# Norm scales of the feed-forwards by two matrix products, copies and offsets of activation rows, and a last down unit by halves, in a two-layer decoder trunk

## Chip, cores and metric

The kernel runs on one core of one Trainium2 chip. The metric is the device time of one execution in microseconds; the median of three runs is quoted. The core's engines are called PE (TensorE), DVE (VectorE), ACT (ScalarE), POOL (GpSimd) and SP (SyncE, which issues nearly all transfers).

## The reference

All of it is float32, with 256 tokens and a width of 1024:

```python
def rms_norm(x, g):
    return x * rsqrt(mean(x * x, axis=-1) + 1e-6) * g

# layer 0
x = x + short_conv_mixer(rms_norm(x, a_norm), ...)      # width-3 causal convolution, gates
x = x + conv_glu_ffn(rms_norm(x, f_norm[0]), ...)       # 1024 -> 2 x 2816 -> 1024
k, v = (rms_norm(x, kv_norm) @ w for w in (w_k, w_v))
# layer 1
x = x + attention(rms_norm(x, b_norm) @ w_q, k, v, rel_bias) @ w_o   # 16 heads of 64, causal
x = x + conv_glu_ffn(rms_norm(x, f_norm[1]), ...)
return rms_norm(x, final_norm)

def conv_glu_ffn(h, w_up, conv_w, conv_b, w_down):
    u = causal_dwconv(h @ w_up, conv_w) + conv_b        # width 3
    g, v = split(u, 2)
    return (silu(g) * v) @ w_down
```

## The kernel before

**Layout and precision.** x is held transposed: 8 row tiles of 128 features by 256 tokens (`xT`). Every float32 matrix product is made of three products in the float32r format: a weight w is split into `hi` (a rounding copy by ACT, L92) and `lo` (the rest, by DVE, L98), an activation into `xh`, `xl` in the same way, and `mm3` (L166) issues wh·xh, wh·xl, wl·xh. Nearly all of PE's work are such products of a 128x128 weight tile with 256 columns. `psum` holds 4 banks `acc` for down projections, 3 banks `up`, and one `misc`.

**Weights** come in units: a big one (`B`, 1 MB) holds two times 8 tiles of an up, query/key or value projection, a small one (`S`, 0.5 MB) a row of a down or output projection. Three raw buffers and three split buffers ("slots") for each size rotate. `hi(tag)` and `lo(tag)` split the next unit in line, whole or by parts; when the last part of a `lo` is done, the load of the unit three further is issued on SP. `hi` is only issued where the slot's previous unit has been used. The order on every engine is the order in which the program is written.

**The norm's scale isn't applied to x.** The products run on x times the gain, and the rows' scale 1/rms is multiplied into the results as they leave PSUM. So PE can start on a new projection before the scale is known. `boundary` (L293) adds the last projection to x, splits x into `xh`, `xl`, squares it on ACT and adds the squares up on DVE to one 128x256 tile `sq[:, 2, :]`. `rstd_cols` (L323) sums that over the partitions with two one-column fp32 products (L327), so that the tokens lie on partitions, and takes the root in three Newton steps on 128x2 (L312 to L317). It makes diagonal matrices of it (L335), and `rstd_rows` (L338) turns those with one fp32 product with a matrix of ones (L341) into a row of 256 scales on every partition, which ACT copies to `rr`. An fp32 product is issued as two in the trace.

**Feed-forward** (`ffn`, L494): 22 units. Unit i multiplies x with its up tiles into a bank of `up` (48 products), `conv` (L498) takes the bank out times `rr` into `u` (DVE, L502), makes the convolution's first tap on ACT (L509) and the other two on DVE (L377), with weight splits between them, and `gate` (L517) makes silu (ACT), `hid` (DVE) and its parts `sh` (ACT) and `sl` (DVE). The `sl` of a unit is issued in the `conv` of the next one, behind its `u` (L504). The down products of unit i (24) stand three units later on PE (L553). Layer 0 has features on the partitions (`down_bank`), layer 1 tokens (`token_bank`: hh·hi, hh·lo, hl·hi). In unit 1 the products run over rows 1, 2, 3, then `rstd_cols`, then the rows 0 and 4 to 7, then `rstd_rows`. Row 0 is taken from a copy, `xh.again`, `xl.again` (`tile_0_again`, L266), that lies 128 bytes into its tile, while the rows themselves begin 192 bytes into a multiple of 512 (`Rows`, L252).

**Attention.** Units v0, v1, v2, q0 to q7, v3 in this order. A query/key unit has products with `xqh` and `xvh` in turn (`qk_step`, L600). Behind every second one a `group` of four heads follows with fp32 scores (L643), softmax, transposes of the group before and its fp32 products with v (L699). The heads' outputs lie in `oh` and `ol`, 8 rows one behind the other (`shifted`, L247). The output projection `wo` has 8 units of 24 products: rows 0 and 1, transposes of the last group, row 2, its products with v, rows 3 to 7.

**The end.** The last unit of layer 1 has its down weights split in `gate(last)`: `hi("S")`, silu, the first half of `lo`, `hid`, `sh`, the second half, `sl`. `token_last` runs the last three units' down products.

Of the kernel before, what the change touches and what calls it, by code (L numbers as in the profile page):

```python
# [17 lines left out]
S = 256  # L18
D = 1024
# [18 lines left out]
def f32(ap):  # L38
    return ap.bitcast(F32)
# [3 lines left out]
def yoco_kernel(ctx: ExitStack, tc: tile.TileContext, t: dict, out: bass.AP):  # L43
# [202 lines left out]

    def shifted(pool, name, tag, rows, **kw):  # L247

        t = pool.tile([128, rows * S + 64], F32R, name=name, tag=tag, **kw)
        return t[:, 48:48 + rows * S].rearrange("p (k s) -> p k s", s=S)  # L250

    class Rows:  # L252
# [7 lines left out]
        def __getitem__(self, i):  # L260
            return self.rows[i]

    def parts_tiles():
        return Rows("xh"), Rows("xl")

    def tile_0_again(xh, xl):  # L266
        A.activation(xh.again, f32(xh[:, 0, :]), AF.Copy)
        V.tensor_copy(xl.again, f32(xl[:, 0, :]))

    def scaled_hi(x, gain, ks, xh, order=same):  # L270
# [67 lines left out]
    def rstd_rows(dg, scales=(1.0,), orders=(same,)):  # L338
# [6 lines left out]
        return r  # L345


    ext_d = dram.tile([NH, 384], F32, name="ext_d")
# [15 lines left out]
    def bias_pair(j):  # L364
# [3 lines left out]
        return b  # L368

    def split_act(src, n, at=64):  # L370

        h, lw = (tmp.tile([128, 384 + 64], F32R, name="s" + x, tag="z" + x, bufs=4)[:, at // 4:at // 4 + n]
                 for x in "hl")
        return (h, lw), lambda: A.activation(h, src, AF.Copy), lambda: V.tensor_sub(lw, src, f32(h))  # L374

# [111 lines left out]
    xh, xl, sq = boundary(acc, xT, P_FN)  # L487
    tile_0_again(xh, xl)
    hi("S")

# [3 lines left out]
    def ffn(layer, xh, xl, sq, bank=down_bank, between=None):  # L494
# [3 lines left out]
        def conv(j, last=False):  # L498
# [6 lines left out]
            if not last:  # L505
                lo("B")
            o = tmp.tile([128, 2, S], F32, name="cv", bufs=2)
# [9 lines left out]
        def gate(j, o, last=False):  # L517
            sl = tmp.tile([128, S], F32, name="sl", tag="sc", bufs=4)
            hi("S")
            A.activation(sl, o[:, 0, :], AF.Silu)  # L520
            lo("S", 0, 1 + last)
            hid = tmp.tile([128, S], F32, name="hid", tag="pr", bufs=4)
            V.tensor_mul(hid, sl, o[:, 1, :])  # L523
            hd[j], zh, low[j] = split_act(hid, S, 64 if layer == 0 else 128)
            zh()
            if last:
                lo("S", 1, 2)
                low[j]()

        acc = None  # L530
        for i in range(FJ):
# [27 lines left out]
            if i == 0:  # L559
                hi("B")  # L560
        if bank is token_bank:
# [9 lines left out]

    xvh, xvl, sq = boundary(acc, xT, P_KVN, rev)
    xqh, xql = parts_tiles()
    vs = wpool.tile([128, 2, D], F32, name="vs", tag="hiB2")
    oh = None
    ol = shifted(act, "ol", "ol", KT, bufs=1)
    vb, qb, qs, sb, pr, pt, ps_, ob, bias = {}, {}, {}, {}, {}, {}, {}, {}, {}
# [21 lines left out]

    def qk_step(j, ks=range(KT)):  # L600
        u = WH["q", j]
        assert u.lo is not None
        wh, wl = u.v(u.hi, 2), u.v(u.lo, 2)
        for k in ks:
            mm3(qb[j][:, 0, :], wh[:, k, 0, :], wl[:, k, 0, :], xqh[:, k, :], xql[:, k, :],
                start=(k == 0), stop=(k == KT - 1))
            mm3(qb[j][:, 1, :], wh[:, k, 1, :], wl[:, k, 1, :], xvh[:, k, :], xvl[:, k, :],
                start=False, stop=(k == KT - 1))
        u.used = ks[-1] == KT - 1
# [128 lines left out]
    for kind, n in heads:  # L738
        if kind == "v":
            vb[n] = acc_bank() if n < 3 else up_bank()  # L740
            if n == 1:
                v_step(1, range(0, 4))
                ycol, dg = rstd_cols(sq)
                v_step(1, range(4, 8))
                oh = shifted(act, "oh", "oh", KT, bufs=1)
            elif n == 2:
# [26 lines left out]
        else:  # L773
            qb[n] = up_bank()
            qk_step(n)
            if n % 2:
# [4 lines left out]
            else:  # L781
                qk_out(n)
                if n:
                    fin[1]()
                hi("B")
                lo("B")
# [27 lines left out]
    xh, xl, sq = boundary(acc, xT, P_FN + KT)  # L814
    tile_0_again(xh, xl)
    hi("S")

# [115 lines left out]
```

## Time and profile before

| | |
|---|---|
| median of 3 runs | 573.8 us (573.79, 573.80, 574.29) |
| profiled execution, its own time | 574.54 us |
| its span, first to last instruction | 572.8 us |
| granted TensorE clock, mean over the span | 0.999 |
| PE, PE's weight loads, DVE, ACT, POOL busy | 98%, 97%, 81%, 58%, 2% of the span |
| products on PE | 4924 |
| read from HBM | 106.65 MB, 188 GB/s over the span |

The profile's instruction times are microseconds from the span's start. A busy share says how long an engine had an instruction in it; matmuls overlap, so PE's share says little of its speed, and the distance from one start to the next is the thing to look at. The chain that ended last is the list of what each step waited for, back from the end.

The span divides into the mixer (to 95.2 us), layer 0's feed-forward (to about 278), values, queries and keys and attention (to 358), the output projection (to 383.9), layer 1's feed-forward (to 566) and the final norm.

### The profile page before, as it was taken

Reading aid. Unit: us, or ns where it says so; the run is one execution under the profiler, and the core shown is the slowest. Engines: PE = TensorE matmul, PEld = TensorE weight load, DVE = VectorE, ACT = ScalarE, POOL = GpSimd, SP = SyncE. Lnnn points to the kernel's source line nnn. Section 1 sums busy time; section 2 is a strip of 40 time slices with the busy share of each in tenths; the row PEclk is TensorE's granted clock in tenths of the full one; section 3 lists DMA queues with packets and bytes.
Section 4 is the critical chain, followed back from the end, with each engine's and each line's share of the span. In section 5 each row is a group of like instructions: output and inputs, shape, how many; then the busy total and the mean of one; then the engine's idle time right before and its main releaser. Section 6 shows DMA issues by size and latency. Waiting matters only on the chain.

```text
span 572.8 us, 11802 instructions
## 1 busy us (share of the span) xinstructions
PE 563.2 (98%) x4924; PEld 557.8 (97%) x4924; DVE 464.8 (81%) x786; ACT 334.6 (58%) x502; POOL 12.2 (2%) x33
## 2 busy tenths in 40 slices
PE   8999999999999999999999999999999999999995
PEld 7999999999999999999999999999999999999994
DVE  5998869888877787777978888658999988888865
ACT  7765437566665566555765666456566556555443
POOL 0410000000000000000000000000000000000001
PEclk9999999999999999999999999999999999999999
DMA  8986583537445644564265655444656554563111
GB/s 286 398 290 218 181 298 112 185 133 264 179 168 215 221 170 168 215 221 156 103 220 196 221 195 189 138 170 148 221 184 221 221 195 162 196 221 129 57 38 73
DMA packets 24180, 108.47 MB, mean 189 GB/s; under 512 B 2736, under 2 KB 5440, under 8 KB 16192
## 3 DMA queue, kind: packets, MB, share of 16 engines
q1 hardware_dynamic: 23840, 107.43, 52.4%
q8 instruction: 38, 0.62, 0.4%
q10 hardware_dynamic: 288, 0.30, 0.2%
q14 instruction: 14, 0.11, 0.1%
HBM read 106.65 MB, written 1.07 MB: 188 GB/s over the span
## 4 chain that ended last, share of the span: by engine, by line
PE 95%; DVE 1%; ACT 1%; DMA 1%; SPq 0%; issue 0%; POOLq 0%; POOL 0%; ACTq 0%
PE up L167 19%; PE up L168 19%; PE up L169 19%; PE acc L167 7%; PE acc L168 7%; PE acc L169 7%; PE acc L198 3%; PE acc L196 3%; PE acc L197 3%; PE up L699 1%; PE acc L588 1%; DMA xres<-xT 1%; PE acc L590 1%; PE acc L591 1%; PE acc L643 1%; DVE loB L98 1%
## 5 line engine op out<-in xcount | busy, mean ns | idle before, releaser
L167 PE MATMUL up<-xh,hiB 128*128 128x256 f32 x944 | 262.2, 278 | 0.7 <-ACT hiB L92 0.6
L169 PE MATMUL up<-xh,loB 128*128 128x256 f32 x944 | 261.1, 277 | 0.5 <-DVE loB L98 0.5
L168 PE MATMUL up<-xl,hiB 128*128 128x256 f32 x944 | 260.9, 276 | 0.0
L167 PEld LDWEIGHTS up<-xh,hiB 128*128 128x128 f32 x944 | 177.2, 188 | 1.6 <-ACT hiB L92 1.1
L169 PEld LDWEIGHTS up<-xh,loB 128*128 128x128 f32 x944 | 177.4, 188 | 0.9 <-DVE loB L98 0.9
L168 PEld LDWEIGHTS up<-xl,hiB 128*128 128x128 f32 x944 | 177.2, 188 | 0.1
L98 DVE TENSOR_TENSOR loB<-rawB,hiB 128x2048 fp32r<-128x2048 f32 (+2 forms) x76 | 147.6, 1948 | 5.3 <-ACT hiB L92 5.0
L92 ACT ACTIVATE hiB<-rawB 128x2048 fp32r<-128x2048 f32 (+1 forms) x73 | 123.5, 1696 | 22.6 <-issue 10.1
L98 DVE TENSOR_TENSOR loS<-rawS,hiS 128x1024 fp32r<-128x1024 f32 (+2 forms) x73 | 83.6, 1146 | 11.5 <-ACT hiS L92 11.2
L509 ACT ACTIVATE cv<-u,pk 128x256 f32<-128x256 f32 x88 | 48.2, 595 | 71.2 <-DVE u L502 71.2
L377 DVE SCALAR_TENSOR_TENSOR cv<-u,pk,cv 128x255 f32<-128x255 f32 x192 | 81.3, 478 | 2.7 <-ACT cv L509 1.7
L92 ACT ACTIVATE hiS<-rawS 128x1024 fp32r<-128x1024 f32 (+1 forms) x71 | 71.6, 1010 | 10.2 <-PE acc L168 6.3
L502 DVE TENSOR_TENSOR u<-up,rr 128x512 f32<-128x512 f32 x44 | 30.3, 689 | 45.2 <-PE up L169 43.8
L169 PE MATMUL acc<-sh,loS 128*128 128x256 f32 x240 | 66.2, 276 | 0.0
L167 PE MATMUL acc<-sh,hiS 128*128 128x256 f32 x240 | 66.2, 276 | 0.0
L168 PE MATMUL acc<-sl,hiS 128*128 128x256 f32 x240 | 66.2, 276 | 0.0
L374 ACT ACTIVATE sh<-hid 128x256 fp32r<-128x256 f32 x52 | 21.7, 417 | 60.0 <-DVE hid L523 55.2
L198 PE MATMUL acc<-hiS,sl 128*128 128x256 f32 x176 | 48.7, 277 | 0.0
L196 PE MATMUL acc<-hiS,sh 128*128 128x256 f32 x176 | 48.7, 277 | 0.0
L197 PE MATMUL acc<-loS,sh 128*128 128x256 f32 x176 | 48.6, 276 | 0.0
L169 PEld LDWEIGHTS acc<-sh,loS 128*128 128x128 f32 x240 | 45.1, 188 | 0.0
L168 PEld LDWEIGHTS acc<-sl,hiS 128*128 128x128 f32 x240 | 45.0, 188 | 0.0
(151 smaller groups left out, 751.9 us busy)
## 6 DMA issues: line engine op xcount, KB each, us to landing
rawB<-w_up SPq DMA_DIRECT2D x44, 1024.0 KB, 4.8
rawS<-w_dn SPq DMA_DIRECT2D x44, 512.0 KB, 3.4
rawB<-w_qk SPq DMA_DIRECT2D x8, 1024.0 KB, 4.8
rawB<-w_mc SPq DMA_DIRECT2D x6, 1024.0 KB, 8.0
rawS<-w_mo SPq DMA_DIRECT2D x8, 512.0 KB, 4.5
rawB<-w_v SPq DMA_DIRECT2D x4, 1024.0 KB, 4.8
rawS<-w_o SPq DMA_DIRECT2D x8, 512.0 KB, 3.6
rawS<-w_mb SPq DMA_DIRECT2D x7, 512.0 KB, 5.3
```

The source lines that it names most:

```text
L92: A.activation(self.hi[:, c], self.raw[:, c], AF.Copy)
L98: V.tensor_sub(self.lo[:, c], self.raw[:, c], f32(self.hi[:, c]))
L167: PE.matmul(o, wh, xh, start=start, stop=False, skip_group_check=True)
L168: PE.matmul(o, wh, xl, start=False, stop=False, skip_group_check=True)
L169: PE.matmul(o, wl, xh, start=False, stop=stop, skip_group_check=True)
L196: PE.matmul(o, hh[:, tok], u.hi[:, f], start=(first and d.start == 0), stop=False, skip_group_check=True)
L197: PE.matmul(o, hh[:, tok], u.lo[:, f], start=False, stop=False, skip_group_check=True)
L198: PE.matmul(o, hl[:, tok], u.hi[:, f], start=False, stop=last, skip_group_check=True)
L374: return (h, lw), lambda: A.activation(h, src, AF.Copy), lambda: V.tensor_sub(lw, src, f32(h))
L377: V.scalar_tensor_tensor(o[:, back:], u[:, :S - back], w, o[:, back:], op0=OP.mult, op1=OP.add)
L502: V.tensor_mul(u, ub[j], rr[:, 0:1, :].to_broadcast([128, 2, S]))
L509: A.activation(o[:, half, :], u[:, half, :], AF.Identity, scale=cw[half][2], bias=par(P_FCB, c0 + half * FJ))
```

## The change

- **`each`**, a 128x128 float32r matrix of 1/1024, 192 bytes into a tile, is made at the start by ACT.
- **`boundary`** with `split` (both feed-forwards; not the keys and values) splits the sum of squares into `sh`, `sl` parts too, and splits the next big unit's `lo` half before, half behind the sums. `tile_0_again` stands in it now.
- **`rstd_direct`** replaces `rstd_cols` and `rstd_rows` in both feed-forwards. Two products with `each` as the stationary tile and the parts as moving ones give the mean of squares in a row on every partition, in `misc`; DVE adds epsilon and takes the root there, with two steps that have other constants: ten operations on 128x256. No ACT copy is left.
- **Unit 1** runs over rows 1 to 6, the norm's two products, the copy of row 0, and row 7.
- **The next big unit** is split by ACT in halves behind unit 0; DVE's first half of `lo` comes before the norm, the second in `conv(0)`.
- **`Heads`** replaces `shifted`: of the heads' output rows, row 3 lies 192 bytes and rows 4 to 7 lie 256 bytes further on.
- **Queries and keys:** behind unit 0's output, row 0 of both inputs is copied, and unit 2 takes row 0 from the copies.
- **The last unit** has ACT's `hi("S")` in two halves, one before and one behind silu.

```diff
+    each = const.tile([128, 192], F32R, name="each")[:, 48:176]
...
+    A.activation(each, ones, AF.Copy, scale=1.0 / D)
...
+    class Heads:
...
+        def __getitem__(self, i):
+            p, j, s = i
...
+            at = 48 + j * S + (48 if j == 3 else 64 if j > 3 else 0)
+            return self.t[p, at:at + S][:, s]
...
-    def boundary(acc, x, gain, order=same):
+    def boundary(acc, x, gain, order=same, split=True):
...
         sum_squares(sq, 0)
-        for part in range(2):
-            lo("B", part, 2)
-        sum_squares(sq, 1, order)
+        if split:
+            lo("B", 0, 2)
+            sum_squares(sq, 1, order)
+            sq, high, low = split_act(sq[:, 2, :], S)
+            high()
+            lo("B", 1, 2)
+            low()
+            tile_0_again(xh, xl)
...
+    def rstd_direct(parts):
+        ps = psum.tile([128, 512], F32, name="misc", bufs=1)
+        PE.matmul(ps[:, :S], each, parts[0], start=True, stop=False, skip_group_check=True)
+        PE.matmul(ps[:, :S], each, parts[1], start=False, stop=True, skip_group_check=True)
+        r = act.tile([128, 2, S], F32, name="rr", bufs=1)
+        w = tmp.tile([128, 2, S], F32, name="u", bufs=2)
+        ms, a, y = w[:, 0, :], w[:, 1, :], r[:, 0, :]
+        V.tensor_scalar(ms, ps[:, :S], EPS, None, op0=OP.add)
+        V.tensor_scalar(y.bitcast(I32), ms.bitcast(I32), -0.5, float(0x5F1FFFF9), op0=OP.mult, op1=OP.add)
+        V.tensor_mul(a, y, y)
+        V.scalar_tensor_tensor(a, a, -0.703952253, ms, op0=OP.mult, op1=OP.mult)
+        V.scalar_tensor_tensor(y, a, 0.703952253 * 2.38924456, y, op0=OP.add, op1=OP.mult)
+        V.tensor_mul(a, y, y)
+        V.tensor_mul(a, a, ms)
+        V.tensor_scalar(ms, a, 0.375, -1.25, op0=OP.mult, op1=OP.add)
+        V.tensor_mul(a, ms, a)
+        V.scalar_tensor_tensor(y, a, 1.875, y, op0=OP.add, op1=OP.mult)
+        return r
...
             if not last:
-                lo("B")
+                lo("B", *((1, 2) if j == 0 else ()))
...
-            hi("S")
+            hi("S", 0, 1 + last)
             A.activation(sl, o[:, 0, :], AF.Silu)
             lo("S", 0, 1 + last)
+            if last:
+                hi("S", 1, 2)
...
-                up_step(up[1], ub[1], xh, xl, 2, range(1, 4), first=1)
-                _, dg = rstd_cols(sq)
+                up_step(up[1], ub[1], xh, xl, 2, range(1, 7), first=1)
+                rr = rstd_direct(sq)
                 lo("S")
                 A.activation(first, ones[:, 0:1], AF.Silu)
-                up_step(up[1], ub[1], xh, xl, 2, (0, 4, 5, 6, 7), first=1, again=True)
-                rr = rstd_rows(dg)
+                up_step(up[1], ub[1], xh, xl, 2, (0, 7), first=1, again=True)
...
             if i == 0:
-                hi("B")
+                for part in range(2):
+                    hi("B", part, 2)
+                hi("S")
+                lo("B", 0, 2)
...
+            for i, (h, lw) in enumerate(((xqh, xql), (xvh, xvl))):
+                h, lw = (h.again, lw.again) if again and k == 0 else (h[:, k, :], lw[:, k, :])
...
-            qk_step(n)
+            qk_step(n, again=n == 2)
...
+                else:
+                    tile_0_again(xqh, xql)
+                    tile_0_again(xvh, xvl)
```

The order of DVE from the sums of squares of layer 0's feed-forward on, before (`nw` holds the root's terms on 128x2, `sq` the squares; two more rounds like the last three rows follow):

```order
L98 TENSOR_TENSOR loB_1313<-rawB,hiB_1161 128x1024 x2
L285 TENSOR_TENSOR sq<-sq 128x512
L287 TENSOR_TENSOR sq<-sq 128x512
L288 TENSOR_TENSOR sq<-sq 128x256
L268 CAST xl<-xl 128x256
L331 TENSOR_SCALAR nw<-misc 128x2
L312 TENSOR_SCALAR nw<-nw 128x2
L314 TENSOR_TENSOR nw<-nw 128x2
L316 SCALAR_TENSOR_TENSOR nw<-nw 128x2
L317 SCALAR_TENSOR_TENSOR nw<-nw 128x2
```

and the same place now, as far as the norm's first operation (`sl<-sq,sh` is the low part of the sum of squares; line numbers are those of the changed kernel):

```order
L98 TENSOR_TENSOR loB_1315<-rawB,hiB_1163 128x1024
L303 TENSOR_TENSOR sq<-sq 128x512
L305 TENSOR_TENSOR sq<-sq 128x512
L306 TENSOR_TENSOR sq<-sq 128x256
L98 TENSOR_TENSOR loB_1315<-rawB,hiB_1163 128x1024
L286 TENSOR_TENSOR sl<-sq,sh 128x256
L280 CAST xl<-xl 128x256
L98 TENSOR_TENSOR loB_1384<-rawB,hiB_1379 128x1024
L384 TENSOR_SCALAR u<-misc 128x256
```

Half a weight split has moved behind the sums, and the low part and half of the next unit's split stand before the norm.

Further on in DVE's order, between the norm and `u` of unit 0, before:

```order
L335 TENSOR_SCALAR dg<-ident,nw 128x128 x2
L98 TENSOR_TENSOR loS_1414<-rawS,hiS_1323 128x1024
L502 TENSOR_TENSOR u<-up,rr 128x512
L98 TENSOR_TENSOR loB_1455<-rawB,hiB_1375 128x2048
L377 SCALAR_TENSOR_TENSOR cv<-u,pk,cv 128x255 x2
```

and now:

```order
L385 TENSOR_SCALAR rr<-u 128x256
L386 TENSOR_TENSOR u<-rr 128x256
L387 SCALAR_TENSOR_TENSOR u<-u 128x256
L388 SCALAR_TENSOR_TENSOR rr<-u,rr 128x256
L389 TENSOR_TENSOR u<-rr 128x256
L390 TENSOR_TENSOR u<-u 128x256
L391 TENSOR_SCALAR u<-u 128x256
L392 TENSOR_TENSOR u<-u 128x256
L393 SCALAR_TENSOR_TENSOR rr<-u,rr 128x256
L98 TENSOR_TENSOR loS_1438<-rawS,hiS_1382 128x1024
L543 TENSOR_TENSOR u<-up,rr 128x512
L98 TENSOR_TENSOR loB_1384<-rawB,hiB_1379 128x1024
```

The root's operations are 256 columns wide, the small unit's split still stands between them and `u`, and only half a big split is left behind `u`. Layer 1 has the same order.

## Rows read from the trace of the kernel before

**Rows 1.** The page, part 4: shares of the chain that ended last, by engine.

```profile
PE 95%; DVE 1%; ACT 1%; DMA 1%; SPq 0%; issue 0%; POOLq 0%; POOL 0%; ACTq 0%
```

**Rows 2.** Stretches: us, busy (instructions) of PE, PEld, DVE, ACT, POOL; PEclk, DMA, GB/s.

```profile
120.00:250.00 130.00, 130.00 (x1149) 130.00 (x1149) 102.66 (x152) 76.94 (x102) 0.00 (x0) 1.00 0.53 194
371.00:383.50 12.50, 12.50 (x108) 12.50 (x107) 6.42 (x10) 5.71 (x7) 0.00 (x0) 1.00 0.64 212
306.60:317.60 11.00, 11.00 (x96) 11.00 (x95) 10.08 (x26) 6.12 (x18) 0.00 (x0) 1.00 0.51 168
```

**Rows 3.** Chain that ended last, units 1 and 2 of layer 0: start, us, what.

```profile
102.85 0.34 PE misc L327 x4
103.19 0.23 PE up L167
...
104.00 0.12 PE up L167
...
104.35 0.11 PE up L167
...
106.73 0.43 PE misc L341 x2
```

**Rows 4.** Timeline of PE, layer 0: start, us, instruction; unit 1's start, first down product.

```profile
100.64 0.28 PE L167 MATMUL up<-xh,hiB 128*128 128x256 f32 x1
...
117.91 0.28 PE L167 MATMUL acc<-sh,hiS 128*128 128x256 f32 x1
```

**Rows 5.** Timeline of DVE, 102 to 115 us, from the norm to unit 0's `sl`.

```profile
103.22 0.16 DVE L331 TENSOR_SCALAR nw<-misc 128x2 f32<-128x2 f32 x1 [0.50 <-PE misc L327]
103.42 0.17 DVE L312 TENSOR_SCALAR nw<-nw 128x2 int32<-128x2 int32 x1
...
107.62 0.69 DVE L502 TENSOR_TENSOR u<-up,rr 128x512 f32<-128x512 f32 x1 [0.61 <-ACT rr L344]
...
110.42 1.66 DVE L377 SCALAR_TENSOR_TENSOR cv<-u,pk,cv 128x255 f32<-128x255 f32 x4
112.23 1.23 DVE L98 TENSOR_TENSOR loS<-rawS,hiS 128x1024 fp32r<-128x1024 f32 x1
...
114.31 0.41 DVE L374 TENSOR_TENSOR sl<-hid,sh 128x256 fp32r<-128x256 f32 x1
```

**Rows 6.** Timeline of ACT, 107 to 114 us, the splits behind the first tap.

```profile
109.34 1.90 ACT L92 ACTIVATE hiB<-rawB 128x2048 fp32r<-128x2048 f32 x1
111.15 1.05 ACT L92 ACTIVATE hiS<-rawS 128x1024 fp32r<-128x1024 f32 x1
```

**Rows 7.** Groups of DVE by shape: count, busy us, mean ns, idle before and releasers.

```profile
L377 DVE SCALAR_TENSOR_TENSOR cv<-u,pk,cv 128x255 f32<-128x255 f32 x96 | 42.8, 479 | 2.4 <-ACT cv L509 1.7 <-ACT cv L415 0.6
...
L523 DVE TENSOR_TENSOR hid<-sl,cv 128x256 f32<-128x256 f32 x44 | 18.5, 419 | 2.2 <-ACT sl L520 2.0
...
L671 DVE TENSOR_SCALAR pr<-pr,st 128x256 f32<-128x256 f32 x16 | 5.6, 351 | 0.3
...
L316 DVE SCALAR_TENSOR_TENSOR nw<-nw 128x2 f32<-128x2 f32 x12 | 1.9, 162 | 0.4
...
L598 DVE TENSOR_SCALAR vs<-acc,nw 128x256 f32<-128x256 f32 x3 | 1.3, 476 | 0.0
```

**Rows 8.** Timeline of PE, units 0 and 1 of layer 1.

```profile
383.85 0.28 PE L167 MATMUL up<-xh,hiB 128*128 128x256 f32 x1
...
391.51 0.28 PE L169 MATMUL up<-xh,loB 128*128 128x256 f32 x1
392.19 0.58 PE L327 MATMUL misc<-ones,sq 128*128 128x1 f32 x4 [0.40 <-DVE sq L288]
```

**Rows 9.** Timelines of ACT and PE at layer 1's last down unit.

```profile
557.31 1.06 ACT L92 ACTIVATE hiS<-rawS 128x1024 fp32r<-128x1024 f32 x1 [0.90 <-PE acc L198]
...
559.72 0.28 PE L198 MATMUL acc<-hiS,sl 128*128 128x256 f32 x1
...
560.42 0.38 PE L198 MATMUL acc<-hiS,sl 128*128 128x256 f32 x1
560.65 0.28 PE L196 MATMUL acc<-hiS,sh 128*128 128x256 f32 x1
```

More of the change, by code (lines that the diff above doesn't have):

```diff
@@ L245, in same @@
         return a
-    def shifted(pool, name, tag, rows, **kw):
-        t = pool.tile([128, rows * S + 64], F32R, name=name, tag=tag, **kw)
-        return t[:, 48:48 + rows * S].rearrange("p (k s) -> p k s", s=S)
     class Rows:
@@ L261, in __getitem__, with __init__ @@
             return self.rows[i]
+    class Heads:
+        def __init__(self, name):
+            self.t = act.tile([128, KT * S + 128], F32R, name=name, bufs=1)
+        def __getitem__(self, i):
+            p, j, s = i
+            if isinstance(j, slice):
+                at = 48 + j.start * S + (64 if j.start > 3 else 0)
+                n = S + 48 if j.start == 2 else S
+                return self.t[p, at:at + 2 * n].rearrange("p (a s) -> p a s", s=n)[:, :, 0:S][:, :, s]
+            at = 48 + j * S + (48 if j == 3 else 64 if j > 3 else 0)
+            return self.t[p, at:at + S][:, s]
     def parts_tiles():
@@ L268, in tile_0_again, with split_act @@
         V.tensor_copy(xl.again, f32(xl[:, 0, :]))
+    def split_act(src, n, at=64):
+        h, lw = (tmp.tile([128, 384 + 64], F32R, name="s" + x, tag="z" + x, bufs=4)[:, at // 4:at // 4 + n]
+                 for x in "hl")
+        return (h, lw), lambda: A.activation(h, src, AF.Copy), lambda: V.tensor_sub(lw, src, f32(h))
     def scaled_hi(x, gain, ks, xh, order=same):
@@ L304, in boundary @@
         sum_squares(sq, 0)
-        for part in range(2):
-            lo("B", part, 2)
-        sum_squares(sq, 1, order)
+        if split:
[8 more added lines that the diff above has]
+            for part in range(2):
+                lo("B", part, 2)
+            sum_squares(sq, 1, order)
         return xh, xl, sq
@@ L368, in bias_pair @@
         return b
[L370 to L374, printed above, removed]
     def tap(o, u, w, back):
@@ L487, in yoco_kernel @@
     xh, xl, sq = boundary(acc, xT, P_FN)
-    tile_0_again(xh, xl)
-    hi("S")
     LAG = 3
@@ L518, in gate @@
             sl = tmp.tile([128, S], F32, name="sl", tag="sc", bufs=4)
-            hi("S")
+            hi("S", 0, 1 + last)
             A.activation(sl, o[:, 0, :], AF.Silu)
             lo("S", 0, 1 + last)
+            if last:
+                hi("S", 1, 2)
             hid = tmp.tile([128, S], F32, name="hid", tag="pr", bufs=4)
@@ L559, in ffn @@
             if i == 0:
-                hi("B")
+                for part in range(2):
+                    hi("B", part, 2)
+                hi("S")
+                lo("B", 0, 2)
         if bank is token_bank:
@@ L569, in yoco_kernel @@
     acc = ffn(0, xh, xl, sq)
-    xvh, xvl, sq = boundary(acc, xT, P_KVN, rev)
+    xvh, xvl, sq = boundary(acc, xT, P_KVN, rev, split=False)
     xqh, xql = parts_tiles()
@@ L575, in yoco_kernel @@
     oh = None
-    ol = shifted(act, "ol", "ol", KT, bufs=1)
+    ol = Heads("ol")
     vb, qb, qs, sb, pr, pt, ps_, ob, bias = {}, {}, {}, {}, {}, {}, {}, {}, {}
@@ L598, in v_out, with qk_step @@
         V.tensor_scalar(vs[:, 1, cols], vb[n][:, 1, :], ycol[:, 1:2], None, op0=OP.mult)
-    def qk_step(j, ks=range(KT)):
+    def qk_step(j, ks=range(KT), again=False):
         u = WH["q", j]
@@ L604, in qk_step @@
         for k in ks:
[L605 to L608, printed above, removed]
+            for i, (h, lw) in enumerate(((xqh, xql), (xvh, xvl))):
+                h, lw = (h.again, lw.again) if again and k == 0 else (h[:, k, :], lw[:, k, :])
+                mm3(qb[j][:, i, :], wh[:, k, i, :], wl[:, k, i, :], h, lw,
+                    start=(k == 0 and i == 0), stop=(k == KT - 1))
         u.used = ks[-1] == KT - 1
@@ L744, in yoco_kernel @@
                 v_step(1, range(4, 8))
-                oh = shifted(act, "oh", "oh", KT, bufs=1)
+                oh = Heads("oh")
             elif n == 2:
@@ L784, in yoco_kernel @@
                     fin[1]()
+                else:
+                    tile_0_again(xqh, xql)
+                    tile_0_again(xvh, xvl)
                 hi("B")
@@ L814, in yoco_kernel @@
     xh, xl, sq = boundary(acc, xT, P_FN + KT)
-    tile_0_again(xh, xl)
-    hi("S")
     xt = act.tile([128, 4, 512], F32, name="xt", tag="ol", bufs=1)
```

## Prediction, made before the changed kernel was run

> **What bounds the kernel now.** I read the page first. TensorE carries 95% of the chain that ended last [rows 1]: nothing is gained beside it, and what counts is how many products it runs, at what pitch, and where it stands still. Hence the busy time by stretches, with the number of products in each [rows 2]. A product occupies the engine for 0.28 us, so a stretch of L us shows those started in L + 0.28. In the feed-forward this gives 130.28/1149 = 0.1134 us from one product to the next; in the output projection 12.78/108 = 0.118, in the third and fourth query/key units 11.28/96 = 0.1175. [...] So there are two pitches, 0.0044 us apart.
>
> The chain of layer 0's first units shows how one turns into the other [rows 3]. After the fp32 column sums (L327) the next product takes 0.23 and those behind it 0.12. At 104.35 they are back at 0.11, a few products after the program has gone from the copy of row 0 to row 4, which lies 64 bytes further in its 512-byte phase. In the two slow stretches no address phase changes, and the slow pitch stays. The timelines of VectorE and ScalarE then say what hangs on the norm, and the last two groups show the two other places where TensorE stands still.
>
> **The change, part by part.** The sum is against the profiled execution, 574.54 us, and 0.7 above the median of the three runs, 573.8; I carry the difference over to the median.
>
> (a) *Layer 0's norm on TensorE.* What goes: the column sums 0.34, the slow restart 0.23 - 0.11 = 0.12, the row product L341 0.43, and about ten slow products 0.04 [rows 3]: 0.94. What comes: two products of 256 columns in the same number format as their neighbours, 0.23. Their operands stand in the address phases of the products around them, and the copy of row 0 follows, so I expect no slow stretch. Saved on TensorE: 0.71.
>
> (b) *Layer 0's norm on VectorE, and who waits.* This is the step that moves work onto the path. Unit 1 starts at 100.64 [rows 4]. With six rows ahead of the norm (36 products, 4.08 us) the two new ones start at 104.72 and 104.84, and VectorE sees the second 0.28 + 0.04 later, at 105.15. Until then VectorE has half a split, the low part and the copy, which end near 104.3; no delay (an estimate from the same operations' lengths before). Then ten dependent operations on 128x256 replace eleven on 128x2 (0.16 each) and the diagonal. Prices: the four tensor-by-tensor ones 0.42; the three with two tensors and constants 0.48 as the taps, or, without a pointer, the 0.16 of their two-column form plus the 0.26 by which 256 columns exceed two, 0.42: I take 0.43; the one that reads PSUM between 0.16 + 0.26 and 0.48: 0.42; the two with one tensor in SBUF 0.35 each, though the integer one could go at one column a cycle, 0.44 [rows 7]. Between dependent ones lie 0.035 (103.22 + 0.16 to 103.42 [rows 5]), nine times. Sum 4.40, bounds 4.35 and 4.7. The chain ends at 109.55. The split of the next down unit comes ahead of `u`, 1.23 less the 0.08 by which independent operations overlap (four taps of 0.48 in 1.66 [rows 5]): `u` of unit 0 starts at 110.6 where it started at 107.62.
>
> Unit 3 needs the bank that `u` frees, and TensorE comes there at 104.95 + 60 products = 111.75; `u` ends at 111.3: no wait, 0.4 to spare. The first down product needs the low part `sl` of unit 0. From `u` to the end of `sl` it takes 114.72 - 107.62 = 7.1 us [rows 5]; the half split that now stands behind `u` doesn't shorten this, since ScalarE binds: the taps' first term, then hiB of 1.90 and hiS of 1.05 [rows 6], and only behind hiS the low split, `hid`, `sh` and `sl`. So `sl` ends at 117.7. Before, it was 114.72 and TensorE wanted it at 118.0 [rows 4, 5]: 3.3 us of cover. Now TensorE arrives at 117.19, and its second product, which reads `sl`, waits from 117.30 to 117.76. The restart costs another 0.11, as behind the wait at 560.42, where 0.38 stands instead of 0.28 [rows 9]. **New wait: 0.57.** By the bounds of the chain 0.5 to 0.87; nothing if ScalarE or VectorE is 0.5 quicker than priced. Net of (a) and (b): 0.94 - 0.23 - 0.57 = 0.14 saved. Later VectorE's lag shrinks: in the steady feed-forward it is busy 102.66 of 130 us [rows 2].
>
> (c) *Layer 1's norm.* Here TensorE also stood still for the sum of squares: from the end of the last product, 391.51 + 0.28, to that of the column sums, 392.19 + 0.58, lie 0.98 [rows 8]. With the slow restart 0.12 and the row product 0.43 as in layer 0, and some 80 products at the slow pitch since 383.85 (0.35), that is 1.88. After: with 36 products instead of 18 ahead of the norm the parts are ready a microsecond early, so no wait there; 0.23 for the two products; and the same VectorE chain. The token-major down products read the low part third instead of second, 0.11 later, so the wait is 0.45. Saved: 1.88 - 0.23 - 0.45 = 1.2.
>
> (d) *Output projection.* Rows 3 to 7 run at the slow pitch. Row 3 now lies 192 bytes on and rows 4 to 7 64 bytes further still, the same step that ends the slow pitch in [rows 3]. So 24 products stay slow and 96 become fast: 96 x 0.0044 = 0.42. Lower bound nothing.
>
> (e) *Query/key units 2 and 3.* Unit 2 starts on the copy, so 6 products stay slow and 90 become fast: 0.40. The four copies fall into unit 1's time, where ScalarE waits for the weights' buffer and VectorE for ScalarE's split: nothing. If that cover were gone, they would take about 0.3 each on their engines.
>
> (f) *Last unit by halves.* hiS (1.06) starts at 557.31 [rows 9] and the gate stands behind it. With half of it ahead, silu, `hid`, `sh` and `sl` come 0.5 earlier. Four products from 559.72 to 560.65 take 0.93 instead of 0.45 [rows 9]; that goes: 0.47, at least 0.3.
>
> (g) *Nothing:* building the constant (one operation of ScalarE while it waits for the first x), the weight splits by halves, the later loads that follow from them (the three raw buffers run units ahead).
>
> Sum: 0.14 + 1.2 + 0.42 + 0.40 + 0.47 = 2.63. **574.54 - 2.6 = 571.9 for the profiled execution, 571.2 against the median.**
>
> **Rivals.** *No new wait:* vector operations or ScalarE's splits are quicker in place; 0.57 + 0.45 come on top: 570.2. For it: the wait is the difference of two long sums, each known to some tenths. Against: every member has a row. 15%.
>
> *A longer wait:* the chain at its upper bound, 0.3 more in each layer, and the end's gain halved: 572.0. 10%.
>
> *The steps in address phase do nothing:* the slow pitch in the two stretches has another cause, and (d), (e) and the 0.35 of (c) fall away: 1.2 less, 572.4. For it: [rows 3] has the copy, but other things changed at the same moment. Against: a few products suffice there, and without a step the pitch stays slow for 12 us. 12%. [...]
>
> *The slow pitch stays (slower than before):* the two products leave TensorE slow, and after the copy's step no address phase changes until the layer's end. From unit 2 on that is 20 x 48 + 22 x 24 = 1488 products, 6.5 us a layer: 573.8 - 2.6 + 6.5 = 577.7 for one layer, 584 for both. It decides when the products behind row 7 of unit 1 still come every 0.118. Against: the new products have their neighbours' format, and a copy has ended the slow pitch behind the worse disturbance of [rows 3]. 6%.
>
> *The change doesn't do what it says at the end:* the waits of the last unit have another cause, 0.47 less: 571.7. 5%.
>
> **How the numbers follow.** The forecast has 52%. A measurement of this kernel tells about 0.2%, 1.15 us, from no change, so faster means below 572.65. The forecast and the rivals up to 572.4 lie there; of the longer waits and the missing steps some part, together or with a further small loss, ends above: faster 0.85, same 0.09, slower 0.06. The range takes in the case without waits at 570.2 and, on the other side, 572.4 and half a microsecond of both faults together: 570.0 to 572.9.
>
> **What would show it.** Right: at both norms the gap of some 0.9 us is replaced by two products 0.11 apart; one wait of 0.3 to 0.9 at the first down product of each layer, released by VectorE's `sl`; 371 to 383 with 110 or more products in 12.5 us; no wait of over 0.1 at the end. Wrong: products every 0.118 us in a feed-forward; a wait at unit 3 for `u`; the ten operations longer than 4.7 us.

## The result and the profile after

The changed kernel takes 581.24 us, the median of 20 runs (574.55 to 588.82). The kernel before took 574.28 beside it (20 runs, 573.79 to 574.94). The medians stand 1.2% apart; the ratio over the runs, six of which stand low, is 1.0087 (1.0067 to 1.0107): slower by 0.9%, where 571.2 and a faster kernel were forecast. Runs over 1.5% above the fastest of their kernel, here the one at 588.82 and in e2 the one at 584.82, are left out of the ratios. The runs don't scatter, they stand on levels: six at 574.55 to 575.74, thirteen at 580.2 to 582.9, one at 588.82. Between the middles of the lower two levels lie 6.5 (574.84 to 581.32), which is what the prediction gave for one layer's products at the slow pitch (1488 x 0.0044); the highest run stands another 7.5 up.

The profiled execution took 581.5 (span 579.7) at a granted clock of 0.998. Its page, part 4:

```profile
PE 86%; DVE 7%; ACT 3%; issue 2%; DMA 1%; SPq 0%; POOLq 0%; POOL 0%; ACTq 0%
```

[Rows 1] had PE 95% and DVE 1%: the end now hangs on VectorE in places. Stretches of the changed kernel (us, busy and instructions of PE, PEld, DVE, ACT, POOL, then clock, DMA, GB/s):

```profile
131.00:250.00 119.00, 119.00 (x1012) 119.00 (x1012) 92.70 (x135) 69.04 (x91) 0.00 (x0) 1.00 0.55 195
313.60:324.60 11.00, 11.00 (x100) 11.00 (x99) 10.36 (x27) 6.00 (x18) 0.00 (x0) 1.00 0.50 162
377.50:390.00 12.50, 12.50 (x112) 12.50 (x111) 6.68 (x11) 5.64 (x7) 0.00 (x0) 1.00 0.64 212
428.00:540.00 112.00, 112.00 (x991) 112.00 (x990) 100.92 (x144) 66.88 (x88) 0.00 (x0) 1.00 0.54 195
```

Layer 0's feed-forward runs at 119.28/1012 = 0.1179 a product at a granted clock of 1.00, where [rows 2] had 0.1134 at the same. Layer 1's, from 428 on, is at 112.28/991 = 0.1133. The third and fourth query/key units (second row, 100 products where there were 96) and the output projection (third row, 112 where there were 108) are fast, as forecast.

TensorE's timeline at the norm, at the first down product, and at unit 5 of each layer (start, us, instruction, idle time and releaser):

```profile
104.58 0.28 PE L379 MATMUL misc<-sh,each 128*128 128x256 f32 x1
104.69 0.28 PE L380 MATMUL misc<-sl,each 128*128 128x256 f32 x1
104.81 0.28 PE L169 MATMUL up<-xh,hiB 128*128 128x256 f32 x1
...
117.09 0.32 PE L169 MATMUL acc<-sh,hiS 128*128 128x256 f32 x1
117.52 0.38 PE L170 MATMUL acc<-sl,hiS 128*128 128x256 f32 x1
117.74 0.28 PE L171 MATMUL acc<-sh,loS 128*128 128x256 f32 x1
...
128.52 0.28 PE L170 MATMUL up<-xl,hiB 128*128 128x256 f32 x1
129.31 0.39 PE L171 MATMUL up<-xh,loB 128*128 128x256 f32 x1 [0.51 <-DVE loB L98]
129.54 0.28 PE L169 MATMUL up<-xh,hiB 128*128 128x256 f32 x1
...
423.74 0.28 PE L170 MATMUL up<-xl,hiB 128*128 128x256 f32 x1
425.70 0.39 PE L171 MATMUL up<-xh,loB 128*128 128x256 f32 x1 [1.69 <-DVE loB L98]
425.93 0.28 PE L169 MATMUL up<-xh,hiB 128*128 128x256 f32 x1
```

The norm is as forecast: two products 0.11 apart, nothing stands still. The first down product's second product comes 0.43 after the first instead of 0.11, and the next one 0.22 later: the forecast wait, 0.43 with its restart. The rest is new. At unit 5 TensorE waits for VectorE's low split of the weights, 0.79 from start to start in layer 0 and 1.96 in layer 1. VectorE's timeline says why:

```profile
105.01 0.42 DVE L384 TENSOR_SCALAR u<-misc 128x256 f32<-128x256 f32 x1 [0.74 <-PE misc L380]
105.47 0.30 DVE L385 TENSOR_SCALAR rr<-u 128x256 int32<-128x256 int32 x1
105.80 0.42 DVE L386 TENSOR_TENSOR u<-rr 128x256 f32<-128x256 f32 x1
...
108.88 0.43 DVE L393 SCALAR_TENSOR_TENSOR rr<-u,rr 128x256 f32<-128x256 f32 x1
109.22 1.22 DVE L98 TENSOR_TENSOR loS<-rawS,hiS 128x1024 fp32r<-128x1024 f32 x1
110.36 0.69 DVE L543 TENSOR_TENSOR u<-up,rr 128x512 f32<-128x512 f32 x1
...
114.97 1.23 DVE L98 TENSOR_TENSOR loS<-rawS,hiS 128x1024 fp32r<-128x1024 f32 x1 [1.21 <-ACT hiS L92]
...
117.05 0.41 DVE L286 TENSOR_TENSOR sl<-hid,sh 128x256 fp32r<-128x256 f32 x1
...
123.09 1.77 DVE L420 SCALAR_TENSOR_TENSOR cv<-u,pk,cv 128x255 f32<-128x255 f32 x4 [0.34 <-ACT cv L550]
125.70 0.43 DVE L566 TENSOR_TENSOR hid<-sl,cv 128x256 f32<-128x256 f32 x1 [0.84 <-ACT sl L561]
...
126.97 2.28 DVE L98 TENSOR_TENSOR loB<-rawB,hiB 128x2048 fp32r<-128x2048 f32 x1
```

The same places in the kernel before, VectorE's:

```profile
120.35 1.77 DVE L377 SCALAR_TENSOR_TENSOR cv<-u,pk,cv 128x255 f32<-128x255 f32 x4 [0.34 <-ACT cv L509]
122.95 0.42 DVE L523 TENSOR_TENSOR hid<-sl,cv 128x256 f32<-128x256 f32 x1 [0.83 <-ACT sl L520]
...
124.22 2.29 DVE L98 TENSOR_TENSOR loB<-rawB,hiB 128x2048 fp32r<-128x2048 f32 x1
```

and TensorE's first product there that reads this split:

```profile
129.01 0.28 PE L169 MATMUL up<-xh,loB 128*128 128x256 f32 x1
```

`u` of unit 0 starts at 110.36, 2.74 later than in [rows 5]; unit 5's low split starts at 126.97, 2.75 later. VectorE has made up nothing in between: the 0.34 and 0.84 that it stands idle in unit 2 it stood idle before too, since ScalarE's tap and silu set the pace there. Before, the split ended at 126.51 and was wanted at 129.01, 2.50 of cover. Now it comes 2.75 later, to a TensorE that is 0.38 earlier: 0.63 missing (measured 0.68: 0.79 from start to start instead of 0.11).

And from 129.89 on products come every 0.118. That lasts to the scores behind the second query/key unit. In layer 1 the three short waits at the first down products (411.99 to 412.67) leave the slow pitch too (87 products from 413 to 423, 10.28/87 = 0.118), and the wait at unit 5 ends it: behind 425.93 the distance falls from 0.120 to 0.113 within five products and stays there. So in this trace one wait left the slow pitch and one the fast.

The starts of the same product in the profiled executions of before and after give the account (us from each span's start). Beside them the same for e10, a version without waits (below):

| place | before | after | after later by | e10 later by |
|---|---|---|---|---|
| ahead of layer 0's norm | 95.89 | 95.74 | -0.14 | +0.05 |
| behind it | 113.14 | 112.33 | -0.81 | -0.62 |
| down products done, ahead of unit 5 | 127.88 | 127.50 | -0.38 | -0.62 |
| in unit 5 | 132.41 | 132.95 | +0.54 | -0.62 |
| behind query/key unit 1 | 304.18 | 311.06 | +6.88 | -0.62 |
| behind query/key unit 3 | 322.46 | 328.93 | +6.48 | -1.02 |
| ahead of layer 1's norm | 389.86 | 395.74 | +5.88 | -1.61 |
| behind it | 401.62 | 406.10 | +4.48 | -3.01 |
| in unit 4, behind the first down products | 411.82 | 416.79 | +4.97 | -3.01 |
| in unit 5, behind its wait | 419.75 | 426.96 | +7.21 | -3.01 |
| ahead of the last unit's down products | 551.22 | 558.43 | +7.21 | -3.01 |
| last down products | 560.76 | 567.54 | +6.78 | -3.44 |

Every gain of the forecast is there (0.67, 0.40, 0.60 + 1.40, 0.43). The waits (0.43, 0.92 with the first slow products behind it, and some 2.3 in layer 1) eat it, and the slow pitch adds 6.3 from layer 0's unit 5 to the scores and, in this execution, 0.4 in layer 1.

### The profile page after: what moved, and what is told of

Same layout as the page of the kernel before. It is cut to its first block, busy times and chain, and to the rows that moved or that the text cites. A ratio compares the mean times of both kernels' runs of the same rounds, so it can differ in the third digit from the quotient of the medians.

```text
span 579.7 us, 11797 instructions
## 1 busy us (share of the span) xinstructions
PE 568.2 (98%) x4916; PEld 562.5 (97%) x4916; DVE 468.9 (81%) x786; ACT 335.7 (58%) x509; POOL 10.3 (2%) x33
## 4 chain that ended last, share of the span: by engine, by line
PE 86%; DVE 7%; ACT 3%; issue 2%; DMA 1%; SPq 0%; POOLq 0%; POOL 0%; ACTq 0%
PE up L171 17%; PE up L169 17%; PE up L170 17%; PE acc L169 6%; PE acc L171 6%; PE acc L170 6%; PE acc L199 3%; PE acc L200 3%; PE acc L198 3%; DVE loB L98 2%; ACT hiB L92 1%; PE up L744 1%; PE acc L633 1%; PE acc L636 1%; PE acc L635 1%
## 5 line engine op out<-in xcount | busy, mean ns | idle before, releaser
L92 ACT ACTIVATE hiB<-rawB 128x2048 fp32r<-128x2048 f32 (+2 forms) x75 | 123.6, 1654 | 20.5 <-issue 9.6
L92 ACT ACTIVATE hiS<-rawS 128x1024 fp32r<-128x1024 f32 (+2 forms) x73 | 72.0, 987 | 10.7 <-PE acc L170 6.8
```

Of the source, the lines that this page charges most:

```text
L92: A.activation(self.hi[:, c], self.raw[:, c], AF.Copy)
```

## The experiments

Three theories. **T1:** VectorE's lateness makes TensorE wait; a wait leaves the pitch slow in some executions, until the next step in address phase. **R1:** the placement of the new tiles sets the pitch. **R2,** the prediction's rival: the norm's two products leave it slow.

**e1, a step in every unit.**

```diff
-                up_step(up[i], ub[i], xh, xl, 2)
+                up_step(up[i], ub[i], xh, xl, 2, again=i > 1)
```

> Edit: every unit of both feed-forwards from unit 2 on takes row 0 from its copy, so each has a step in address phase. T1 (VectorE's long root makes TensorE wait at the first down product and again at unit 5's low split; a wait leaves the pitch slow at random, until the next step): the waits stay (about 0.4 and 0.8 in layer 0, 0.6 and 2.0 in layer 1), but no stretch keeps 0.118 longer than a unit, 3 us; every run lies at 574.5 to 575.5, where the best runs of the changed kernel lie, none over 577. R1 (the pitch is set by something else than waits and steps, placement of the new tiles for instance): the runs stay a mixture about 581 and stretches of 100 us and more at 0.118 stay.

576.70 us median, 576.46 to 578.87 (6 runs), ratio 1.0047 (1.0033 to 1.0061). No run stands 6.5 higher, and the longest stretch at 0.118 in its trace, behind a wait of 2.3 at layer 1's unit 5, ends with the step of the next unit:

```profile
420.50:427.00 6.50, 6.50 (x58) 6.50 (x57) 6.29 (x11) 4.20 (x6) 0.00 (x0) 1.00 0.45 164
429.50:436.00 6.50, 6.50 (x60) 6.50 (x59) 6.47 (x10) 4.33 (x6) 0.00 (x0) 1.00 0.58 198
```

But all runs lie above the 575.5 at which T1's range ended, five by 1.0 to 1.6 and one by 3.4: steps aren't free. In

```profile
131.00:250.00 119.00, 119.00 (x1046) 119.00 (x1046) 94.49 (x137) 69.63 (x92) 0.00 (x0) 1.00 0.57 206
```

119.28/1046 is 0.1140, 0.0007 over the fast pitch. That is 0.05 for the 72 products of a unit, 2 us for 40 units.

**e2, the small split behind unit 0's taps.**

```diff
                 rr = rstd_direct(sq)
-                lo("S")
...
-                gate(0, conv(0))
+                o = conv(0)
+                lo("S")
+                gate(0, o)
```

> Edit: the small weight split that stands between the root and `u` of unit 0 moves behind the taps of unit 0, where VectorE stood idle 1.2 us. T1: `u` starts 1.1 earlier, no wait at the first down product of layer 0 nor at unit 5's low split there, layer 1's wait at unit 5 falls from 2.0 to about 0.8 or less; layer 0 keeps 0.1134 in all runs; best runs at 572 to 572.8, some runs 6.5 higher by layer 1 alone. R1 (placement): the waits shrink, 1 to 2 us faster, but the mixture with steps of 6.5 stays in layer 0 too. R2 (the two products of the norm leave the pitch slow): the same as R1.

573.24 us median (12 runs): eight at 572.63 to 573.47, three at 578.2 to 579.8, one at 584.82; ratio 1.0009 (0.9980 to 1.0038). The wait at the first down product is gone, and the levels begin 2 us lower. T1 expected that layer 0 would never be slow; the run at 584.8, some two levels up, would need that, but it has no trace. A wait is left in layer 0's unit 5:

```profile
128.29 0.28 PE L170 MATMUL up<-xl,hiB 128*128 128x256 f32 x1
128.49 0.39 PE L171 MATMUL up<-xh,loB 128*128 128x256 f32 x1
```

0.20 from start to start, of which 0.09 is waiting. Layer 1's unit 5 still has 1.73, and in the profiled run, one of the low ones, both waits leave the pitch fast (119.28/1053 and 112.28/991, both 0.1133). Four of twelve runs stand higher where it was fourteen of twenty: too few to say that shorter waits do it less often.

**e3, the change without its norm.** The norms as before; `each`, `Heads`, the copies and the last unit stay.

```diff
-    xh, xl, sq = boundary(acc, xT, P_FN)
+    xh, xl, sq = boundary(acc, xT, P_FN, split=False)
+    tile_0_again(xh, xl)
+    hi("S")
...
-                rr = rstd_direct(sq)
+                _, dg = rstd_cols(sq)
...
```

> Edit: both feed-forwards' norms as in the kernel before (column sums, diagonal, row product, the old order of the splits); the copies and offsets in attention and the last unit by halves stay, and so does the constant's tile, so that the tiles lie where the changed kernel has them. T1: none of the waits, no slow feed-forward; all runs at 572.8 to 573.2, which is 574.3 less the 1.3 forecast for the three other parts (0.42, 0.40, 0.47). R1 (placement of the new tiles): runs near 580 here too. If the three parts bring nothing: 574.3.

573.51 us (572.82 to 574.25, 11 runs), ratio 0.9985 (0.9977 to 0.9994). No run near 580: R1 falls for the tiles' placement. But 0.7 was gained instead of 1.3. Its trace gives two causes. The third and fourth query/key units are slow in spite of the copy, 96 products as in [rows 2]:

```profile
306.60:317.60 11.00, 11.00 (x96) 11.00 (x95) 9.95 (x27) 5.95 (x17) 0.00 (x0) 1.00 0.50 165
```

and what the output projection gains is half lost at layer 1's old norm, where TensorE, earlier now, waits 0.70 for the sum of squares instead of 0.4:

```profile
391.67 0.58 PE L355 MATMUL misc<-ones,sq 128*128 128x1 f32 x4 [0.70 <-DVE sq L306]
```

Comparing the starts of the same products with those before: 0.01 lost in the query/key units, 0.65 gained from there to the last product ahead of the norm's sums, 0.28 given back in the wait for them and 0.09 behind it, 0.44 gained in the last unit: 0.71 in all.

**e4, the norm alone.** No `Heads` offsets, no copies for queries and keys, last unit as before.

```diff
...
-            at = 48 + j * S + (48 if j == 3 else 64 if j > 3 else 0)
+            at = 48 + j * S
...
-            hi("S", 0, 1 + last)
+            hi("S")
...
-            qk_step(n, again=n == 2)
+            qk_step(n)
...
```

> Edit: the norms as in the changed kernel, without the offsets of the heads' rows, without the copies for queries and keys, last unit as before. T1: the changed kernel's waits and its mixture, all levels 1.3 higher: best runs 575.9, most 582.4. If the three other parts have a hand in the slow pitch: all runs below 577.

582.67 us, all four runs within 582.56 to 582.75, ratio 1.0144 (1.0131 to 1.0157): the changed kernel's upper level plus 1.3. The slow pitch comes with the norm and needs nothing of the rest. Its output projection, without offsets, is slow again (x109, for x112 above; third row: layer 1, from behind the norm to unit 5):

```profile
131.00:250.00 119.00, 119.00 (x1013) 119.00 (x1012) 92.69 (x134) 69.01 (x91) 0.00 (x0) 1.00 0.53 195
377.50:390.00 12.50, 12.50 (x109) 12.50 (x108) 6.42 (x10) 5.70 (x7) 0.00 (x0) 1.00 0.64 212
403.00:424.00 21.00, 21.00 (x180) 21.00 (x180) 18.47 (x33) 11.22 (x17) 0.00 (x0) 1.00 0.54 193
```

The third row shows more than was asked. The slow pitch of the output projection runs on through layer 1's norm, through the copy of row 0 and through the step to row 7 (21.28/180 = 0.118), and ends at the wait at unit 5, 1.81 from start to start (991 products from 428 to 540, 0.1133). The same step in address phase that ended it in e1 did nothing here. In the kernel before, layer 1's slow pitch ended behind the copy too, but there TensorE had also waited for the sums [rows 8].

**e5, a wait alone, in the kernel before.**

```diff
-            V.tensor_mul(u, ub[j], rr[:, 0:1, :].to_broadcast([128, 2, S]))
+            for _ in range(7 if layer == 0 and j == 3 else 1):
+                V.tensor_mul(u, ub[j], rr[:, 0:1, :].to_broadcast([128, 2, S]))
```

> Edit, in the kernel before: unit 3's output of layer 0 (`u`, 0.60 us each behind one another) is computed seven times instead of once, which does nothing but hold VectorE up by 3.6 us, so that the low split of unit 5 ends at about 130.1 and TensorE, which wants its second half near 128.6, stands still for about 1.2 us. The norm is untouched. T1: a plain wait suffices to leave the pitch slow: some of the runs lie at about 575.4, some 6.5 higher, with 0.118 from the wait to the next step in address. R2 (only the norm's new products, or the new placement, do it): all runs at 574.3 to 575.6.

Five runs at 575.66 to 577.12, one at 582.09, which is the profiled one (ratio 1.0038, 1.0025 to 1.0051). VectorE's delay, TensorE's timeline at the wait, and the stretches ahead of and behind it:

```profile
122.78 5.04 DVE L503 TENSOR_TENSOR u<-up,rr 128x512 f32<-128x512 f32 x7
```

```profile
128.37 0.28 PE L168 MATMUL up<-xl,hiB 128*128 128x256 f32 x1
130.40 0.39 PE L169 MATMUL up<-xh,loB 128*128 128x256 f32 x1 [1.75 <-DVE loB L98]
```

```profile
110.00:126.00 16.00, 16.00 (x144) 16.00 (x143) 14.38 (x26) 7.95 (x13) 0.00 (x0) 1.00 0.47 165
131.00:250.00 119.00, 119.00 (x1013) 119.00 (x1012) 92.57 (x135) 68.35 (x90) 0.00 (x0) 1.00 0.55 195
314.70:325.70 11.00, 11.00 (x99) 11.00 (x99) 10.40 (x27) 6.00 (x18) 0.00 (x0) 1.00 0.49 160
```

The delay is 5.04 less 0.68, more than reckoned, and so is the wait. The pitch is 16.28/144 = 0.1131 ahead and 119.28/1013 = 0.1177 behind, with the old norm and none of the new tiles. None of the 67 runs of the kernel before that were measured beside the versions stands above 575.5. A plain wait of VectorE's making suffices, in one run of six; R2 isn't needed. The last row is a by-product: query/key units 2 and 3 are fast here *without* a copy (11.28/99 = 0.114).

**e6, half a root.** The second step of the root is left out, so the scale is only a first approximation.

```diff
-        V.tensor_mul(a, y, y)
-        V.tensor_mul(a, a, ms)
-        V.tensor_scalar(ms, a, 0.375, -1.25, op0=OP.mult, op1=OP.add)
-        V.tensor_mul(a, ms, a)
-        V.scalar_tensor_tensor(y, a, 1.875, y, op0=OP.add, op1=OP.mult)
```

> Edit, in the changed kernel: the root's second step is left out (five of the ten vector operations, 2.3 us less), which leaves the scale at its first approximation; the two products and everything else stay. T1: no wait at the first down product nor at unit 5 in layer 0, at most a few tenths in layer 1; layer 0 never slow; best runs 3.0 below the changed kernel's, 571.2 to 572. R2 (the products leave the pitch slow): 0.118 in the feed-forwards and levels 6.5 apart in layer 0 too.

572.33 us (571.04 to 574.01, 7 runs), ratio 0.9966 (0.9954 to 0.9978). No wait in layer 0, one of 0.59 from start to start at layer 1's unit 5, both layers fast in the trace: with the same two products on TensorE and 2.3 us less on VectorE no run stands 6.5 higher. Five of the seven lie above the 572 expected, four of them by under 0.5, one by 2, which its time alone doesn't explain.

**e7, cover and one step.** On top of e2:

```diff
-            if between and 2 <= i < 18:
-                between(i - 2)
+            if between and 5 <= i < 21:
+                between(i - 5)
...
-                up_step(up[i], ub[i], xh, xl, 2)
+                up_step(up[i], ub[i], xh, xl, 2, again=i == 6)
```

> Edit, in the changed kernel: the small split behind the taps of unit 0 as in e2; the 16 transposes of x on VectorE that stand behind units 2 to 17 of layer 1 (0.69 each) stand behind units 5 to 20, which takes two of them from ahead of unit 5's low split; and unit 6 of each layer, and it alone, takes row 0 from its copy. T1: waits of about 0.2 in layer 0 and 0.1 to 0.5 in layer 1; a slow pitch behind them ends at unit 6; all runs at 571.7 to 572.6, none 6.5 higher. If one step doesn't end it: some runs at 578.

572.63 us (572.30 to 573.25, 8 runs), ratio 0.9974 (0.9964 to 0.9984): faster than both kernels, and no run 6.5 higher. It lies at the upper end of what was expected because only one transpose stood ahead of layer 1's split, not two: the wait there fell from 1.73 to 1.17 from start to start, by 0.56.

**e8, the root on GpSimd.**

```diff
...
-        V.tensor_scalar(y.bitcast(I32), ms.bitcast(I32), -0.5, float(0x5F1FFFF9), op0=OP.mult, op1=OP.add)
...
+        G.tensor_tensor(y, ms, half.to_broadcast([128, S]), op=OP.pow)
...
```

> Edit, in the changed kernel: VectorE only adds epsilon, and GpSimd raises 128x256 means to the power -0.5 in one operation; the small split that follows on VectorE runs beside it; transposes and unit 6's step as in e7. GpSimd's power on 128x1 takes 0.57 in the final norm, and its copies of 16x144 take 2.6, or 0.018 a column; so between 0.6 and 5 us here, 3 taken. T1: with 3 us VectorE is free for the split (1.2) meanwhile, `u` starts 0.4 earlier than with e2's order, VectorE has 4 us less to do, no waits: 570.8 to 571.6. At 5 us `u` comes at the time it has in the changed kernel, with a wait at the first down product and none at unit 5: 571.5 to 572.5.

649.59 us, ratio 1.1329 (1.1297 to 1.1360). The price was wrong by far, 41.6 us for one operation instead of 3 (groups of GpSimd: busy us, mean ns):

```profile
L388 POOL TENSOR_TENSOR rr<-u,each 128x256 f32<-128x256 f32 x2 | 83.1, 41570 | 362.8 <-DVE u L387 362.8
```

41.57/256 is 0.16 a column; the 0.018 of the copies did not foretell it. TensorE stands still for it, 36.9 and 36.1 us from start to start, and the mean granted clock of the execution is 0.943, where the changed kernel had 0.998. Later the pitch is fast in both layers of the profiled run, and stays so behind a wait of 0.78 at layer 1's unit 5: the run takes 78.1 more than e10's (649.2 to 571.1), 72.5 of it waiting for the two roots, and the 5.6 left are less than one layer's 6.5. Neither the long waits nor the short one left it slow.

**e9 and e10, the split into the gap,** on top of e7; e10 is e9 without unit 6's step.

```diff
-                lo("B", *((1, 2) if j == 0 else ()))
+                lo("B", *((1, 2) if j in (0, 3) else ()))
...
+            if j == 2:
+                lo("B", 0, 2)
             return o
```

> Edit, on top of e7: in both layers the first half of unit 5's low split is issued at the end of unit 2's taps, where VectorE stood idle 0.84 for silu, the second half behind unit 3's output as before. e7 left waits of 0.10 (layer 0) and 1.06 (layer 1) at this split beyond the pitch. T1: 1.14 of work leaves the place and `hid` of unit 2 comes about 0.35 later, so the wait in layer 0 goes and that in layer 1 falls to about 0.3; with the restart 0.1 that is 0.9 below e7's 572.6: 571.7, no run over 573. If VectorE's lateness is not what TensorE waits for there: 572.6.

> Edit: e9 without the step at unit 6. T1: layer 0 has no wait left, so it keeps 0.1134 in every run; layer 1 has a wait of about 0.3, so some runs may lie 6.5 higher, but none 13; the others at 571.6. If something other than waits turns the pitch slow: levels 6.5 and 13 higher, as in e2.

e9: 571.21 us (570.62 to 571.44), ratio 0.9946 (0.9934 to 0.9958). e10: 571.10 (570.58 to 571.88), ratio 0.9945 (0.9932 to 0.9959). Five runs each, none higher. The half split lies where VectorE stood idle, and `hid` of unit 2 follows it without idle time (VectorE, e9, layer 1):

```profile
412.00 1.23 DVE L98 TENSOR_TENSOR loB<-rawB,hiB 128x1024 fp32r<-128x1024 f32 x1 [0.54 <-ACT hiB L92]
413.14 0.42 DVE L568 TENSOR_TENSOR hid<-sl,cv 128x256 f32<-128x256 f32 x1
```

No gap between TensorE's products is left in the first six units of either layer, and with nothing to wait for the pitch is fast without any step (e10, 0.1133 in both rows):

```profile
131.00:250.00 119.00, 119.00 (x1053) 119.00 (x1052) 95.26 (x138) 70.48 (x93) 0.00 (x0) 1.00 0.56 204
428.00:540.00 112.00, 112.00 (x991) 112.00 (x990) 98.91 (x145) 64.37 (x86) 0.00 (x0) 1.00 0.50 179
```

e10 has the norm's two products, the ten operations, `each`, `Heads` and the copies, as the changed kernel has them. It differs in the order of VectorE's work alone, with one split cut in two. That decides for T1 against R1 and R2 on where the slow pitch comes from (that a step ends it holds in some places only, e1 and e4), and it is a version that beats both kernels by 0.5% and more.

## Why the prediction was wrong

**Two steps failed. The first is the end of (b),** "Later VectorE's lag shrinks: in the steady feed-forward it is busy 102.66 of 130 us". An average over a stretch was put where a chain was wanted. VectorE's spare time in units 1 and 2 is time in which it waits for ScalarE, and none of it came back: lag 2.74 at `u`, 2.75 at unit 5. Cover was reckoned at two places, the bank for unit 3 and the first down product. The third, unit 5's split with 2.50 of cover, wasn't looked up, though its rows stood in the trace of before. Worth 0.92 in layer 0, the first slow products included, and, with the slow products ahead of it, 2.2 in layer 1.

**The second, the larger one: a wait was priced at its length and a restart of 0.11.** Its other price is a slow pitch, 0.1179 for 0.1133, until something ends it: the next wait in layer 1 (0.120 to 0.113), a step in some places; from layer 0 it lasted to the scores. That is 6.3 in the profiled run from layer 0's unit 5 to the scores, and in fourteen of twenty runs a level above the lowest. The sum held a wait in each layer and no such term. The prediction's slower rival named the effect, its size (6.5) and two levels (577.7 and 584, where 581.3 and 588.8 were measured), at 6%. Its cause was wrong. Behind the norm's products some ten come slowly, 104.81 to 105.76, the six of the copy and the first of row 7, and from there the pitch is fast up to the waits; and e10 keeps the two products and stands high in none of its five runs. It also said that the matter is decided behind row 7 of unit 1, where all was well.

**What held.** (a) 0.71 forecast, 0.67 measured. In (b) the ten operations take 4.30 from the first's start to the last's end, 4.40 forecast; `u` at 110.36 for 110.6, `sl` done at 117.46 for 117.7, the wait 0.43 for 0.57. (c) and (d) together, without the wait, 2.07 forecast (1.88 - 0.23 + 0.42) and 2.00 measured (6.48 to 4.48). The waits at layer 1's first down products take 0.34, 0.49 with the slow products behind them, for 0.45. (f) 0.47 forecast, 0.43 measured. Two sums are off as written, by too little to matter: (a)'s terms give 0.93, not 0.94, and 109.55 with 1.23 less 0.08 is 110.7, not 110.6.

**(e) was right in the profiled run by chance.** Over all profiled kernels, query/key units 2 and 3 were fast in five with the copies (after, e1, e8, e9, e10) and slow in four (e2, e3, e6, e7); without copies they were slow in two (before, e4) and fast in one (e5). In all nine with copies most products on the copy itself are slow; behind it the pitch is fast in five (11.28/100 = 0.113 in the changed kernel) and stays slow in four (11.28/96 = 0.1175 in e3). Whether the copy ends a slow pitch in the five, or the scores ahead had left a fast one, these traces don't show. Why a step works in some places and not in others (here, and in e4's layer 1) wasn't settled.

**(d)'s step did work,** in every trace: with the heads' offsets rows 5 to 7 came at 0.1133 in all nine, and row 4, in which the pitch changes, at 0.1147; without them rows 4 to 7 came at 0.1178 in all three. That answers the rival of steps that do nothing, for this place. There are 112 and 109 products in 12.5 us, with the same shape and clock (1.00), and the same program at this place but for the rows' offsets.

**Put together again:** without waits the change is worth 3.1 us by the medians, 574.23 to 571.10, and 3.44 by the profiled executions, 574.54 to 571.10, where the forecast's rival "no new wait" had 3.65 (2.63 + 0.57 + 0.45). The 3.44 have (e)'s 0.40 in them, which other traces lack.

What stays open: what decides which pitch a wait leaves (thirteen of twenty runs of the changed kernel stand one level up, one of six in e5, all four in e4), whether a longer wait does it more often, in which layer the runs without a trace were slow, and what within TensorE or its feed the slow pitch is.

## What to carry to other kernels

When work moves onto an engine that others wait for, follow its lag consumer by consumer until it has been absorbed, with the cover of each read from the trace; idle time in which that engine waits for a third one absorbed nothing here (0.34 and 0.84 of it in unit 2, and the lag went from 2.74 to 2.75). A move in its order is then often the remedy: here the same work in another order on VectorE made 581 into 571. And where a kernel's runs stand on levels instead of scattering, divide the step by a count of instructions before looking for anything else: 6.5 over 1488 products was the distance of two pitches that the trace of before had side by side.

## What the hardware showed that was not expected

- Products of equal shape at a granted clock of 1.00 run for 100 us and more at 0.1133 or at 0.1178 a product, and waits of TensorE switched from one to the other in both directions (the changed kernel: 0.79 from start to start in layer 0, 0.1179 behind it; 1.96 in layer 1, 0.120 to 0.113). Others didn't: 0.20 and 1.73 from start to start left it fast in e2's trace (0.1133), 36.9 and 36.1 in e8's.
- A step in the address phase of the moving rows went with the fast pitch in some places (the output projection, 0.1133 behind it in nine of nine traces, 0.1178 without it in three of three; layer 1's unit 6 in e1, 58 and then 60 products in 6.5 us) and not in others (the query/key units, fast in five of nine; layer 1's norm in e4, 0.118), and a short use of a row at another phase costs some 0.05 us itself (estimated from e1's 0.1140 for 0.1133 over the 72 products of a unit).
- GpSimd's power on 128x256 took 41.57 us, 0.16 a column (e8).
